# Opening of a two-block layer kernel on one core: x transposed before its norm, smaller first weight tiles, warm-up products

## The chip, the cores and the metric

The kernel runs on one core of a Trainium2 chip. The metric is the device time of one execution in microseconds (us). The core's engines are TensorE (PE, matrix products; its weight loads are listed as PEld), VectorE (DVE), ScalarE (ACT), GpSimd (POOL) and the queue of SyncE (SP), which here issues every transfer from memory. Each engine works through its own list of instructions in order and waits at an instruction until what it needs is there.

## The reference

A block of 256 tokens with 1024 features passes through two decoder layers and a second, different block. Only the start of the first layer bears on this change:

```python
def rmsnorm(x, g):
    y = xf * lax.rsqrt(jnp.mean(xf * xf, axis=-1, keepdims=True) + EPS)
    return (y * g).astype(x.dtype)
...
proj = rmsnorm(h, g_norm) @ w_in                # 1024 -> 6144
q, k, v, gate = jnp.split(proj, ...)            # 4 heads
q = rotary(heads(q, RET_QK_DIM), pos)
k = rotary(heads(k, RET_QK_DIM), pos) * (RET_QK_DIM ** -0.5)
o = retention_chunkwise(q, k, heads(v, RET_V_DIM))
...
y = (jax.nn.silu(gate) * o_normed) @ w_out
return h + y
...
gate = jax.nn.sigmoid(rmsnorm(h, g) @ w_gate)   # per layer embedding
return h + gate * (p_i @ w_emb)
```

The second block needs cosines and sines of the token positions (`positions_2`), which have nothing to do with the first layer.

## The kernel before, in words

All weights come from memory in tiles of up to 1 MB, in the order of a list (`make_plan`, L117). `Tile` (L161) issues a tile's load on the SP queue into one of three raw buffers; `split` (L173) cuts a half of it into two float32r parts, `hi` by ScalarE (L178) and `lo = raw - hi` by VectorE (L179), into one of four buffers each. A product of float32 accuracy is then three matmuls, hi*hi, hi*lo, lo*hi (`mm_A`, L250 to L255, 512 columns each). `gen_A` (L257) runs such products with tokens on the partitions and K outermost, two token halves to a weight tile; `ahead` (L197) splits the next tile's halves meanwhile. `gen_B` (L230) makes results with features on the partitions.

TensorE's order is the order of the program (`manual_schedule`, L278). The order of the other engines' lists is chosen when the program is built, by a scheduler, except inside blocks that name ScalarE and VectorE as manual too.

The opening goes so. `p`, two tiles of `ple_w_emb`, `x` in two halves of 128 tokens and the first tile of `ret_w_in` are asked for (L288 to L297, L171), then the tables `c_cos`, `c_sin`, `c_dec` (L617, L618). TensorE transposes `p` (`embed_T`, L413). `normed_all` (L388) takes the mean squares of `x`, one half on ScalarE (L392) and one on VectorE (L393); GpSimd turns each into 1/sqrt (`rstd`, L334: an add, L335, and a power, L336); VectorE multiplies `x` by it (L397). `embed` (L424) runs the 24 products p @ w_emb, and between its third and last quarter TensorE transposes the normed `x` (16 transposes, L362), which `split_psum` with the gain (L350, L351) brings into the operand `X`. Then come the gate and values of head 0 (L613: 96 matmuls, four 1 MB tiles), its queries and keys (`col_q`, `col_k`, L620), whose evacuation `ret_rope` (L476) multiplies by the tables `cs`, and the other heads.

`angles` (L556) is called after head 1's products. It loads the positions and the inverse frequencies (`posi`, L560; `inv`, L564) and reduces the angles on GpSimd: 45 small instructions, L562 to L591.

Of the kernel before, what the change touches and what calls it, by code (L numbers as in the profile page):

```python
# [17 lines left out]
P = 128  # L18
BIG = 1.0e30
T = 256  # L20
# [5 lines left out]
class Units:  # L26
    """4 KB per-partition slots; a freed slot is taken again in the order of release."""
# [31 lines left out]
class TPair:  # L59
    """A transposed operand [K = 4*128 per unit][tokens] as its two float32r parts."""  # L60
# [16 lines left out]
def build(nc, tc, A, out, stage=99):  # L77
# [27 lines left out]
    # ---------------------------------------------------------------- weights  # L105
    # The weights come in tiles of up to 1 MB, in the order of PLAN. A tile is loaded ahead of its
    # use and split into two float32r parts, hi + lo = the float32 value exactly.
# [9 lines left out]
    def make_plan():  # L117
        for n in range(2):
            plan_A("ple_w_emb", 0, [n * 512], 2, 2)
        plan_A("ret_w_in", 0, [4096, 2048])  # L120
# [40 lines left out]
    class Tile:  # L161
        """A tile of weights; h(k), l(k): the two parts of its K tile k"""

        def __init__(self, spec):
            key, lay, k0, nk, c0, ncol = self.spec = spec
            ap = A[key] if lay is None else A[key][lay]
            self.m, self.ncol, self.per = nk * ncol // 2, ncol, nk // 2
            self.hs, self.ls = [], []
            self.raw = wp.tile([P, 2048], F, tag="raw", bufs=3, name=nm("raw"))
            rv = self.raw[:, :nk * ncol].rearrange("p (k n) -> p k n", k=nk)  # L170
            nc.sync.dma_start(rv, ap[k0 * P:(k0 + nk) * P, c0:c0 + ncol].rearrange("(k p) n -> p k n", p=P))  # L171
# [25 lines left out]
    def ahead():  # L197
        """split one half more of the tile that comes next"""
# [21 lines left out]
    # Products come as generators that stop after every 6 matmuls of 512 columns (or 12 of 256),  # L220
    # so that other work of the tensor engine can be put in between.
# [8 lines left out]
    def gen_B(x, ap, c0, evac, ntiles=2, nk=8):  # L230
        """out[ntiles * 128 columns on partitions][256 tokens], two tiles to a bank; evac(i, bank)"""
# [25 lines left out]
    def gen_A(x, cols, evac, nk=8, kt=4):  # L257
        """out[tokens][512 columns of each (ap, c0)], K tiles outermost; evac(i, half, bank)"""
        ps = [[acc(), acc()] for _ in cols]
        for k0 in range(0, nk, kt):  # L260
            last = k0 + kt >= nk
            for i, (ap, c0) in enumerate(cols):
# [5 lines left out]
                for j, (k, h) in enumerate(order):  # L268
# [3 lines left out]
                    if j % 2 == 1:  # L272
                        if j // 2 in LOOK:
                            ahead()
# [5 lines left out]
    # ---------------------------------------------------------------- constants  # L280
# [10 lines left out]
    pn0 = embed_load(A["p"][0, 0])  # L291
    vret = cp.tile([8, P], F, name="vret")
    nc.sync.dma_start(vret, A["ret_norm"].rearrange("l (k p) -> (l k) p", p=P))
    loaded(2)
    nat = [U.get(), U.get()]
    for h in range(2):
        nc.sync.dma_start(nat[h].t, A["x"][0, h * P:(h + 1) * P, :])  # L297
# [35 lines left out]
    # ---------------------------------------------------------------- shared pieces  # L333
# [4 lines left out]
    def sumsq(src, dst, n):  # L338
        """dst[p] = mean over n of src^2, for the piece given"""
# [13 lines left out]
    def transpose_cols(src, kts, dsts):  # L353
        """src(h, k) -> [128 tokens, 128 columns]; dsts: list of (TPair, gcol or None)"""
# [21 lines left out]
    def normed(src, ss, eps):  # L376
        """src divided by its root mean square; ss: per half, the mean squares of its two pieces"""
# [10 lines left out]
    def normed_all(src, eps):  # L388
        """as normed, the sums of squares of the halves on two engines"""
        xn = [U.get(), U.get()]  # L390
        ss, rs = [small(1), small(1)], [small(1), small(1)]
        nc.scalar.activation(xn[0].t, src[0].t, AF.Square, scale=1.0 / 32.0, accum_out=ss[0])  # L392
        nc.vector.scalar_tensor_tensor(xn[1].t, src[1].t, 1.0 / 1024.0, src[1].t, OP.mult, OP.mult, accum_out=ss[1])  # L393
        for h in range(2):
            rstd(rs[h], ss[h], eps)
            for c in range(2):
                nc.vector.tensor_scalar(xn[h].t[:, c * 512:(c + 1) * 512], src[h].t[:, c * 512:(c + 1) * 512],  # L397
                                        rs[h], None, OP.mult)
        return xn

    class Flat:
        """An operand of up to two K tiles held in one unit, float32r parts side by side"""
# [21 lines left out]
    def embed(pu, w_ap, mid=None):  # L424
        """p @ w_emb, natural, two units; mid() goes before the last quarter of the products"""
# [22 lines left out]
    # ================================================================ retention  # L448
    with tc.manual_schedule(engines={mybir.EngineType.Activation, mybir.EngineType.DVE}):
        pu = embed_T(pn0)  # L450
        for i in range(4):
            queue[i // 2].split()
        vectors_T()
        xn = normed_all(nat, 1e-6)
    X = TPair(U, 8)
    emb = embed(pu, ("ple_w_emb", 0), lambda: transpose_cols(
        lambda h, k: xn[h].t[:, k * P:(k + 1) * P], list(range(8)), [(X, gcol("ret"))]))
    for u in xn:
        u.free()
# [4 lines left out]
    def ret_gv(hd):  # L464
        """evacuation of the gate (column group 0) and the values (1) of a head"""
# [3 lines left out]
        def gate(i, h, ps):  # L469
            nc.scalar.activation(sg.t[:, h * 512:(h + 1) * 512], ps, AF.Silu)  # L470

        def val(i, h, ps):
            split_psum(ps, vh.t[:, h * 512:(h + 1) * 512], vl.t[:, h * 512:(h + 1) * 512])
# [1009 lines left out]
```

## Time and profile before

| | |
|---|---|
| median of 3 runs | 891.42 us (891.24 to 891.92) |
| the profiled execution's own time | not listed with it; its span, first to last instruction, is 889.4 us |
| TensorE busy | 866.6 us, 97% of the span |
| VectorE, ScalarE, GpSimd busy | 620.4, 522.5, 68.4 us |
| mean rate of the transfers | 174 GB/s |

The span leaves out what lies before the first and after the last instruction; the median of the runs is 2.0 us above it. In the timeline each row is one instruction or a run of like ones: start, duration, engine, line, operation, result and inputs, count, and in brackets the idle time of its engine before it with what ended it. A matmul's duration includes its passage through the array, so the rate is read from the distance of two starts.

### The profile page before, as it was taken

How to read it: one execution, taken by the hardware profiler on the slowest of the kernel's cores; microseconds unless marked ns; L12 is line 12 of the kernel's file. 1: busy time of each engine (PE TensorE's matmuls, PEld its weight loads, DVE VectorE, ACT ScalarE, POOL GpSimd, SP SyncE). 2: the span in 40 equal slices, each digit the busy share in tenths (PEclk: the TensorE clock that was granted, in tenths of full speed). 3: DMA queues.
4: the chain of work that ended last, by engine and by line, in shares of the span. 5: the costliest groups of instructions: out<-in, count | busy, mean ns of one | idle time of the engine just before them, and what ended most of it. 6: DMA issues, size and time to landing. Idle time of an engine off the chain costs nothing.

```text
span 889.4 us, 14303 instructions
## 1 busy us (share of the span) xinstructions
PE 866.6 (97%) x5579; PEld 782.9 (88%) x5579; DVE 620.4 (70%) x1078; ACT 522.5 (59%) x948; POOL 68.4 (8%) x152
## 2 busy tenths in 40 slices
PE   6999999999999999999999999999999999999995
PEld 5889898888789999988988888787789999999994
DVE  5577677775687866887777656897857475446665
ACT  6554455454775767976968546647954545444441
POOL 2270000000100000000000000000023000000002
PEclk9999999999999999999999999999999999999998
DMA  8754545644466787425143553746455546655541
GB/s 284 239 190 150 182 148 171 220 143 166 156 212 190 231 298 238 118 78 180 55 143 114 176 187 128 236 150 218 154 160 173 190 142 191 202 184 190 182 142 48
DMA packets 115525, 154.69 MB, mean 174 GB/s; under 512 B 4737, under 2 KB 77826, under 8 KB 115458
## 3 DMA queue, kind: packets, MB, share of 16 engines
q1 hardware_dynamic: 115458, 153.78, 52.6%
q8 instruction: 44, 0.72, 0.3%
q14 instruction: 23, 0.19, 0.1%
HBM read 152.72 MB, written 1.05 MB: 173 GB/s over the span
## 4 chain that ended last, share of the span: by engine, by line
PE 62%; issue 3%; ACT 3%; DVE 2%; POOL 1%; POOLq 0%; ACTq 0%
PE acc L240 11%; PE acc L241 11%; PE acc L242 11%; PE acc L255 6%; PE acc L253 6%; PE acc L254 6%; ACT n L1159 1%; PE tps L1025 1%; ACT whi L178 1%; PE acc L796 1%; PE acc L795 1%; PE tps L362 1%; DVE wlo L179 1%; PE tps L1190 1%; PE acc L1012 1%
## 5 line engine op out<-in xcount | busy, mean ns | idle before, releaser
L179 DVE TENSOR_TENSOR wlo<-raw,whi 128x1024 fp32r<-128x1024 f32 (+1 forms) x284 | 339.0, 1201 | 169.2 <-ACT whi L178 168.4
L178 ACT ACTIVATE whi<-raw 128x1024 fp32r<-128x1024 f32 (+1 forms) x284 | 293.4, 1040 | 221.7 <-PE acc L241 99.8
L240 PE MATMUL acc<-n,whi 128*128 128x256 f32 x960 | 273.3, 285 | 0.0
L242 PE MATMUL acc<-n,wlo 128*128 128x256 f32 x960 | 271.7, 283 | 0.0
L241 PE MATMUL acc<-n,whi 128*128 128x256 f32 x960 | 271.5, 283 | 0.0
L253 PE MATMUL acc<-whi,n 128*128 128x512 f32 x568 | 225.6, 397 | 2.8 <-ACT whi L178 2.8
L254 PE MATMUL acc<-wlo,n 128*128 128x512 f32 x568 | 222.7, 392 | 0.3 <-DVE wlo L179 0.3
L255 PE MATMUL acc<-whi,n 128*128 128x512 f32 x568 | 222.4, 391 | 0.0
L241 PEld LDWEIGHTS acc<-n,whi 128*128 128x128 f32 x960 | 184.1, 192 | 0.6
L240 PEld LDWEIGHTS acc<-n,whi 128*128 128x128 f32 x960 | 183.9, 192 | 0.4
L242 PEld LDWEIGHTS acc<-n,wlo 128*128 128x128 f32 x960 | 184.0, 192 | 0.2 <-DVE wlo L179 0.2
L253 PEld LDWEIGHTS acc<-whi,n 128*128 128x128 f32 x568 | 107.4, 189 | 25.0 <-ACT whi L178 2.9
L255 PEld LDWEIGHTS acc<-whi,n 128*128 128x128 f32 x568 | 107.2, 189 | 23.1 <-DVE n L351 0.4
L254 PEld LDWEIGHTS acc<-wlo,n 128*128 128x128 f32 x568 | 107.4, 189 | 22.2 <-DVE wlo L179 1.2
L347 ACT ACTIVATE n<-tmp 128x512 fp32r<-128x512 f32 (+1 forms) x32 | 19.7, 615 | 40.5 <-DVE tmp L1017 11.9
L335 POOL TENSOR_SCALAR sm<-sm 128x1 f32<-128x1 f32 (+1 forms) x26 | 8.8, 337 | 421.9 <-DVE sm L1413 195.7
L980 ACT ACTIVATE n<-n,sm 128x16 f32<-128x16 f32 (+2 forms) x96 | 37.6, 393 | 0.8 <-DVE sm L978 0.4
L350 ACT ACTIVATE n<-tps,colv 128x256 fp32r<-128x256 f32 x64 | 27.1, 480 | 11.4 <-PE tps L362 6.3
L351 DVE SCALAR_TENSOR_TENSOR n<-tps,colv,n 128x256 fp32r<-128x256 f32 x64 | 28.0, 477 | 2.3 <-ACT n L350 1.8
L348 DVE TENSOR_TENSOR n<-tmp,n 128x512 fp32r<-128x512 f32 (+1 forms) x32 | 21.8, 681 | 10.0 <-ACT n L347 9.6
L348 DVE TENSOR_TENSOR n<-tps,n 128x512 fp32r<-128x512 f32 x31 | 20.6, 685 | 6.4 <-ACT n L347 6.2
L347 ACT ACTIVATE n<-tps 128x512 fp32r<-128x512 f32 x31 | 17.6, 591 | 10.5 <-PE tps L1025 6.1
(246 smaller groups left out, 845.9 us busy)
## 6 DMA issues: line engine op xcount, KB each, us to landing
raw<-in_w_in_dram SPq DMA_DIRECT2D x36, 1024.0 KB, 4.9
raw<-in_ret_w_in_dram SPq DMA_DIRECT2D x24, 1024.0 KB, 5.1
raw<-in_nsa_w_in_dram SPq DMA_DIRECT2D x16, 1024.0 KB, 5.2
raw<-in_kv_w_dram SPq DMA_DIRECT2D x12, 1024.0 KB, 5.0
raw<-in_ret_w_out_dram SPq DMA_DIRECT2D x8, 1024.0 KB, 4.9
raw<-in_ple_w_gate_dram SPq DMA_DIRECT2D x8, 1024.0 KB, 5.1
raw<-in_nsa_w_out_dram SPq DMA_DIRECT2D x8, 1024.0 KB, 5.1
raw<-in_cmp_w_k_dram SPq DMA_DIRECT2D x4, 1024.0 KB, 5.5
```

Source lines behind the costliest of these rows:

```text
L178: nc.scalar.activation(hi[:, :m], src, AF.Copy)
L179: nc.vector.tensor_tensor(lo[:, :m], src, hi[:, :m], OP.subtract)
L240: mm(o, wh, x.hi(k), start=(k == 0), stop=False)
L241: mm(o, wh, x.lo(k), start=False, stop=False)
L242: mm(o, wl, x.hi(k), start=False, stop=(k == nk - 1))
L253: mm(ps, xh, wh, start=start, stop=False)
L254: mm(ps, xh, wl, start=False, stop=False)
L255: mm(ps, xl, wh, start=False, stop=stop)
L347: nc.scalar.activation(hi, src, AF.Copy)
L348: nc.vector.tensor_tensor(lo, src, hi, OP.subtract)
L351: nc.vector.scalar_tensor_tensor(lo, src, scale, hi, OP.mult, OP.subtract)
L980: nc.scalar.activation(dst, dst, AF.Exp, bias=mx[:, i:i + 1], scale=-1.0, accum_out=sums[:, b * 3 + i:b * 3 + i + 1])
```

## The change

`normed_all` goes. `x` is transposed as it comes (`x_T`), its gain still applied when the transposes are brought out. The factor 1/rms of each token (`rsr`) is applied where it can be afterwards: as `scale` of the gate's Silu and of the values' evacuation, for all four heads, and for queries and keys by multiplying it into the tables `cs`. For that `rsr` is spread over 128 columns by VectorE (L665), transposed by TensorE (L666), and multiplied into `cs` (L668). The two mean squares are taken later, in the midst of head 0's products (L647, L648). The embedding's weights come as two tiles of one K tile each; head 0's gate and value weights as eight tiles of 0.5 MB (`kt=2`) in place of four of 1 MB. Five products of the identity with itself stand ahead of `embed_T` and three behind it (`warm`). The tables and small vectors are asked for behind the fifth 0.5 MB tile. Core of the diff:

```diff
-        for n in range(2):
-            plan_A("ple_w_emb", 0, [n * 512], 2, 2)
-        plan_A("ret_w_in", 0, [4096, 2048])
+        PLAN.extend(("ple_w_emb", 0, k, 1, 0, 1024) for k in range(2))
+        plan_A("ret_w_in", 0, [4096, 2048], kt=2)
...
-                        if j // 2 in LOOK:
+                        if kt == 2 or j // 2 in LOOK:
                             ahead()
...
+    with tc.manual_schedule(engines={mybir.EngineType.SP}):
+        pn0 = embed_load(A["p"][0, 0])
+        loaded(1)
+        nc.sync.dma_start(vret, A["ret_norm"].rearrange("l (k p) -> (l k) p", p=P))
+        for h in range(2):
+            nc.sync.dma_start(nat[h].t, A["x"][0, h * P:(h + 1) * P, :])
+        loaded(3)
+    def warm(n):
+        t = tps()
+        for i in range(n):
+            mm(t[:, i % 4 * P:(i % 4 + 1) * P], ident, ident, start=True, stop=True)
...
+    def x_T():
+        banks = [tps() for _ in range(4)]
+        for h in range(2):
+            for k in range(8):
+                c = k % 2 * 256 + h * P
+                nc.tensor.transpose(banks[k // 2][:, c:c + P], nat[h].t[:, k * P:(k + 1) * P], ident)
+        def evac(i):
+            for j in range(2):
+                k = 2 * i + j
+                split_psum(banks[i][:, j * 256:(j + 1) * 256], X.hi(k), X.lo(k), gcol("ret")(k))
+        return evac
...
-            nc.scalar.activation(sg.t[:, h * 512:(h + 1) * 512], ps, AF.Silu)
+            nc.scalar.activation(sg.t[:, h * 512:(h + 1) * 512], ps, AF.Silu, scale=rsr[:, h:h + 1])
-            split_psum(ps, vh.t[:, h * 512:(h + 1) * 512], vl.t[:, h * 512:(h + 1) * 512])
+            split_psum(ps, vh.t[:, h * 512:(h + 1) * 512], vl.t[:, h * 512:(h + 1) * 512], rsr[:, h:h + 1])
...
+    t = gen_A(X, [(wi, 4096), (wi, 2048)], lambda i, h, ps: (g, v)[i](i, h, ps), kt=2)
+    with tc.manual_schedule(engines={mybir.EngineType.Activation, mybir.EngineType.DVE}):
+        warm(5)
+        pu = embed_T(pn0)
+        warm(3)
+        ps = [[acc(), acc()], [acc(), acc()]]
+        def emb_out(n):
+            for h in range(2):
+                nc.scalar.activation(emb[h].t[:, n * 512:(n + 1) * 512], ps[n][h], AF.Copy)
+        for k in range(2):
+            if k:
+                vectors_T()
+                evac = x_T()
+                evac(0)
+                evac(1)
+                queue[0].split()
+                evac(2)
+                queue[0].split()
+                evac(3)
+            w = load_w("ple_w_emb", 0, k, 1, 0, 1024)
+            for n in range(2):
+                for h in range(2):
+                    mm_A(ps[n][h], Flat(pu), k, h, w.h(n), w.l(n), k == 0, k == 1)
+        ahead()
+        emb_out(0)
+        ahead()
+        emb_out(1)
+        adv(t, 5)
+        ss = [small(1), small(1)]
+        j = [U.get(), U.get()]
+        nc.scalar.activation(j[0].t, nat[0].t, AF.Square, scale=1.0 / 32.0, accum_out=ss[0])
+        nc.vector.scalar_tensor_tensor(j[1].t, nat[1].t, 1.0 / 1024.0, nat[1].t, OP.mult, OP.mult, accum_out=ss[1])
+        for h in range(2):
+            j[h].free()
+            rstd(rsr[:, h:h + 1], ss[h], 1e-6)
+    pu.free()
+    adv(t, 2)
...
+    with tc.issue_after(queue[-1].dma.ins):
...
+    run(t)
+
+    rb, rp = tmp(), tps()
+    for h in range(2):
+        nc.vector.tensor_copy(rb[:, h * P:(h + 1) * P], rsr[:, h:h + 1].to_broadcast([P, P]))
+        nc.tensor.transpose(rp[:, h * P:(h + 1) * P], rb[:, h * P:(h + 1) * P], ident)
+    for i in range(2):
+        nc.vector.tensor_tensor(cs[:, i, :], cs[:, i, :], rp[:, :256], OP.mult)
```

Three lists show where the scheduler puts things now. First the SP queue, from its first transfer; `n_..` are the 4 KB units (`p`, `x`, tables), `raw_..` the weight tiles. Before:

```order
L288 DMA n_1_82<-in_p_dram 128x2x256
L293 DMA vret<-in_ret_norm_dram 8x128
L171 DMA raw_86<-in_ple_w_emb_dram 128x2x512
L171 DMA raw_88<-in_ple_w_emb_dram 128x2x512
L297 DMA n_2_90<-in_x_dram 128x1024
L297 DMA n_3_91<-in_x_dram 128x1024
L171 DMA raw_218<-in_ret_w_in_dram 128x4x512
L617 DMA n_16_380<-in_c_cos_dram 128x256
```

and in the change:

```order
L288 DMA n_3_87<-in_p_dram 128x2x256
L171 DMA raw_89<-in_ple_w_emb_dram 128x1024
L296 DMA vret<-in_ret_norm_dram 8x128
L298 DMA n_1_82<-in_x_dram 128x1024
L298 DMA n_2_83<-in_x_dram 128x1024
L171 DMA raw_94<-in_ple_w_emb_dram 128x1024
L171 DMA raw_96<-in_ret_w_in_dram 128x2x512
L563 DMA posi<-in_positions_dram 128x2x1
L567 DMA inv<-in_c_inv_dram 128x32
L171 DMA raw_241<-in_ret_w_in_dram 128x2x512
```

The positions and inverse frequencies moved up from the 25th and 26th place of the queue to the 8th and 9th, straight behind the first 0.5 MB tile.

GpSimd, behind the constants that it sets up at the start: `sm_..` are the two mean squares and their 1/sqrt, L562 on is `angles`. Before:

```order
L335 TENSOR_SCALAR sm_131<-sm_129 128x1
L336 TENSOR_TENSOR sm_131<-sm_131,mhalf 128x1
L335 TENSOR_SCALAR sm_132<-sm_130 128x1
L336 TENSOR_TENSOR sm_132<-sm_132,mhalf 128x1
L562 CAST posf<-posi 128x2
L568 TENSOR_SCALAR n_28_900<-inv,posf 128x32 x2
```

In the change `CAST posf<-posi` (L565) follows the constants directly, the 45 instructions of `angles` run in one piece, and their last two rows stand ahead of the 1/sqrt:

```order
L590 TENSOR_TENSOR trig<-trig,n_28_956 128x64
L594 TENSOR_SCALAR trig<-trig 128x64
L343 TENSOR_SCALAR rsr<-sm_291 128x1
L344 TENSOR_TENSOR rsr<-rsr,mhalf 128x1
L343 TENSOR_SCALAR rsr<-sm_292 128x1
L344 TENSOR_TENSOR rsr<-rsr,mhalf 128x1
```

The two pieces changed places: the 1/sqrt of `x` came before `angles` and now comes after all of it.

VectorE in the change, in head 0's gate and value products; `raw_96`, `raw_241`, `raw_263`, `raw_285`, `raw_318`, `raw_354` are the first to sixth of the eight 0.5 MB tiles, two splits each:

```order
L179 TENSOR_TENSOR wlo_266<-raw_263,whi_265 128x512
L179 TENSOR_TENSOR wlo_276<-raw_263,whi_275 128x512
L179 TENSOR_TENSOR wlo_288<-raw_285,whi_287 128x512
L648 SCALAR_TENSOR_TENSOR n_15_294,sm_292<-n_2_83 128x1024
L179 TENSOR_TENSOR wlo_309<-raw_285,whi_308 128x512
L179 TENSOR_TENSOR wlo_321<-raw_318,whi_320 128x512
L665 COPY tmp_442<-rsr 128x128 x2
L179 TENSOR_TENSOR wlo_345<-raw_318,whi_344 128x512
L179 TENSOR_TENSOR wlo_357<-raw_354,whi_356 128x512
```

The two copies that spread `rsr`, which the program writes behind head 0, stand between the two splits of the fifth tile. From the end of head 0 on, the lists of all engines are those of before, but for the scaled evacuations of the four heads, the two transposes (L666) and the two products into `cs` (L668).

## Rows read from the trace of the kernel before

**Rows 1.** The page's head and part 1: busy us (share of span), instructions of each engine.

```profile
span 889.4 us, 14303 instructions
...
PE 866.6 (97%) x5579; PEld 782.9 (88%) x5579; DVE 620.4 (70%) x1078; ACT 522.5 (59%) x948; POOL 68.4 (8%) x152
```

**Rows 2.** TensorE's waits in 0 to 80 us: line, releaser, us in total, times, longest.

```profile
PE tps L419 <- DMA n<-in_p_dram: 3.7, 1, 3.7
...
PE acc L253 <- ACT whi L178: 2.8, 1, 2.8
```

**Rows 3.** TensorE's timeline: start us, us, engine, line, operation, out<-in, count.

```profile
7.85 0.80 PE L253 MATMUL acc<-whi,n 128*128 128x512 f32 x1 [2.83 <-ACT whi L178]
...
8.57 0.80 PE L254 MATMUL acc<-wlo,n 128*128 128x512 f32 x1
...
13.01 0.63 PE L255 MATMUL acc<-whi,n 128*128 128x512 f32 x1
...
13.44 0.49 PE L253 MATMUL acc<-whi,n 128*128 128x512 f32 x1
...
14.93 1.91 PE L362 MATMUL tps<-ident,n 128*128 128x128 f32 x16
...
18.05 0.39 PE L253 MATMUL acc<-whi,n 128*128 128x512 f32 x1
...
18.73 0.39 PE L253 MATMUL acc<-whi,n 128*128 128x512 f32 x1
...
40.49 0.28 PE L240 MATMUL acc<-n,whi 128*128 128x256 f32 x1
```

**Rows 4.** The SP queue's issues in the timeline.

```profile
5.79 0.58 SPq L617 DMA_DIRECT2D n<-in_c_sin_dram  x1
...
32.59 0.50 SPq L560 DMA_DIRECT2D posi<-in_positions_dram  x1
```

**Rows 5.** Transfers issued in 0 to 60 us: size, us from issue to landing.

```profile
n<-in_c_sin_dram SPq DMA_DIRECT2D x1, 128.0 KB, 8.5
...
posi<-in_positions_dram SPq DMA_DIRECT2D x1, 1.0 KB, 4.7
```

**Rows 6.** GpSimd's timeline: the piece `angles` and a later 1/sqrt.

```profile
37.39 0.71 POOL L562 CAST posf<-posi 128x2 f32<-128x2 int32 x1 [23.30 <-DMA posi<-in_positions_dram]
...
39.64 0.24 POOL L576 CAST n<-ni 128x64 f32<-128x64 int32 x1
...
40.70 1.11 POOL L579 CAST n<-ni 128x64 f32<-128x64 int32 x1
...
52.20 1.27 POOL L576 CAST n<-ni 128x64 f32<-128x64 int32 x1
...
59.37 1.36 POOL L586 TENSOR_SCALAR n<-n 128x64 f32<-128x64 f32 x1
...
63.81 0.43 POOL L591 TENSOR_SCALAR trig<-trig 128x64 f32<-128x64 f32 x1
...
71.02 0.22 POOL L335 TENSOR_SCALAR sm<-sm 128x1 f32<-128x1 f32 x1 [6.78 <-DVE sm L526]
...
71.33 0.57 POOL L336 TENSOR_TENSOR sm<-sm,mhalf 128x1 f32<-128x1 f32 x1
```

**Rows 7.** VectorE's timeline: splits, a sum of squares, a copy.

```profile
7.83 2.65 DVE L179 TENSOR_TENSOR wlo<-raw,whi 128x512 fp32r<-128x512 f32 x4 [1.66 <-ACT whi L178]
...
11.07 1.25 DVE L393 SCALAR_TENSOR_TENSOR n<-n 128x1024 f32<-128x1024 f32 x1 [0.52 <-DMA n<-in_x_dram]
...
52.15 1.23 DVE L179 TENSOR_TENSOR wlo<-raw,whi 128x1024 fp32r<-128x1024 f32 x1 [0.20 <-ACT whi L178]
...
54.49 0.21 DVE L327 COPY colv<-tps 128x57 f32<-128x57 f32 x1
```

**Rows 8.** Stretches: length, busy PE, PEld, DVE, ACT, POOL (instructions), clock granted, DMA share, GB/s.

```profile
880.00:881.00 1.00, 0.35 (x2) 0.00 (x0) 0.67 (x2) 0.00 (x0) 0.34 (x1) 1.00 0.00 0
...
885.00:886.00 1.00, 0.00 (x0) 0.00 (x0) 0.00 (x0) 0.00 (x0) 0.70 (x1) 0.50 0.00 0
```

More of the change, by code (lines that the diff above doesn't have):

```diff
@@ L166, in __init__ @@
             ap = A[key] if lay is None else A[key][lay]
-            self.m, self.ncol, self.per = nk * ncol // 2, ncol, nk // 2
+            self.m, self.ncol, self.per = nk * ncol // 2, min(ncol, 512), max(nk // 2, 1)
             self.hs, self.ls = [], []
@@ L170, in __init__ @@
             rv = self.raw[:, :nk * ncol].rearrange("p (k n) -> p k n", k=nk)
-            nc.sync.dma_start(rv, ap[k0 * P:(k0 + nk) * P, c0:c0 + ncol].rearrange("(k p) n -> p k n", p=P))
+            self.dma = nc.sync.dma_start(rv, ap[k0 * P:(k0 + nk) * P, c0:c0 + ncol].rearrange("(k p) n -> p k n", p=P))
         def split(self):
@@ L289, in embed_load @@
         return pn
-    pn0 = embed_load(A["p"][0, 0])
+    nat = [U.get(), U.get()]
     vret = cp.tile([8, P], F, name="vret")
[L293 to L297, printed above, removed]
+    with tc.manual_schedule(engines={mybir.EngineType.SP}):
[9 more added lines that the diff above has]
+            mm(t[:, i % 4 * P:(i % 4 + 1) * P], ident, ident, start=True, stop=True)
     vecs = cp.tile([P, P], F, name="vecs")
@@ L386, in normed @@
         return xn
[L388 to L399, printed above, removed]
     class Flat:
@@ L446, in dump @@
         es.close()
[L449 to L454, printed above, removed]
-    X = TPair(U, 8)
[L456 to L459, printed above, removed]
+    X = TPair(U, 8)
+    emb = [U.get(), U.get()]
+    rsr = cp.tile([P, 2], F, name="rsr")
+    def x_T():
[9 more added lines that the diff above has]
+        return evac
     wi = ("ret_w_in", 0)
@@ L612, in build @@
     g, v = ret_gv(0)
-    run(gen_A(X, [(wi, 4096), (wi, 2048)], lambda i, h, ps: (g, v)[i](i, h, ps)))
+    t = gen_A(X, [(wi, 4096), (wi, 2048)], lambda i, h, ps: (g, v)[i](i, h, ps), kt=2)
[33 more added lines that the diff above has]
+            rstd(rsr[:, h:h + 1], ss[h], 1e-6)
@@ L614, in build @@
+    pu.free()
+    adv(t, 2)
     cs_u, dec_u = U.get(), U.get()
     cs, dec = cs_u.v(2, 256), dec_u.v(4, 256)
-    for i, c in enumerate(("c_cos", "c_sin")):
-        nc.sync.dma_start(cs[:, i, :], A[c])
-    nc.sync.dma_start(dec, A["c_dec"].rearrange("h p n -> p h n"))
-    vectors2_load()
+    with tc.issue_after(queue[-1].dma.ins):
+        for i, c in enumerate(("c_cos", "c_sin")):
+            nc.sync.dma_start(cs[:, i, :], A[c])
+        nc.sync.dma_start(dec, A["c_dec"].rearrange("h p n -> p h n"))
+        vectors2_load()
```

## The prediction, made before any run of the change

> **What bounds the kernel now.** The page first: TensorE is busy 866.6 of 889.4 us [rows 1], so a change pays only where it moves TensorE. The waits of TensorE come next: in the first 80 us it waits 3.7 us for `p` and 2.8 us for the first split weights [rows 2], and hardly at all for anything else. In its timeline [rows 3] the reader is to see three points. The embedding starts at 7.85 us and runs from 8.57 us on. From 8.57 to 13.44 us eleven matmuls of 512 columns take 4.87 us, a start every 0.43 us, which is 1.2 GHz; later three starts take 0.68 us (18.05 to 18.73), 0.227 us each, the level of 2.4 GHz. Eleven at that pace take 2.5 us, so the low clock costs 2.4 us. Head 0's gate and value products (96 matmuls) start at 18.05 us, and its queries at 40.49 us. That second point is my yardstick, because from there on TensorE's list is the same in both kernels, apart from two transposes.
>
> **What the change sets out to do** is to fill the idle time before 7.85 us, and to take the sums of squares, the 1/sqrt and the multiplication out of the way of X. None of those held TensorE up for long: it has work from 8.57 to 18.05 us. At the very most the change gains the 2.4 us of low clock and the 0.6 us that head 0 now takes beyond 96 x 0.227 = 21.8 us.
>
> **What it adds.** The lists above decide. GpSimd now runs all of `angles` before the 1/sqrt of `x`, and VectorE has the two copies of `rsr` between the two splits of the fifth 0.5 MB tile of head 0. VectorE works in order: at the first copy it stands until GpSimd has done `angles` and the 1/sqrt, and behind it stands the second `lo` part of the fifth tile, which TensorE needs. So I add up when that part is ready.
>
> 1. *The positions arrive.* On the one queue transfers land in the order of their issue. Before, 2308 KB (p, the norm gain, two embedding tiles, x) are through when VectorE takes the second half of x at 11.07 us [rows 7]. The sines, 1280 KB later in the queue, are issued at 5.79 us and land 8.5 us later, at 14.3 us [rows 4, 5]: 512 KB take 1.3 us. The change puts 2820 KB ahead of the positions, so these come at about 11.07 + 1.3 = 12.4 us, and the first instruction of `angles` starts at 12.5 us. The positions' own transfer is small (4.7 us from issue to landing before, behind a tile).
>
> 2. *`angles` itself.* Before, it runs from 37.39 to 64.24 us, 26.85 us for 45 instructions [rows 6]. Eight of them take 1.05 to 1.36 us, 9.9 us in all, where the same operations take 0.24 to 0.37 us elsewhere (L576: 1.27 us at 52.20, 0.24 us at 39.64). The one at 52.20 us lies beside VectorE's split of 52.15 to 53.38 us and ends just behind it [rows 7]; the other seven lie so too. Each costs 0.93 us, so a split of 1.23 us costs GpSimd its length less 0.3 us. Without these 7.4 us, 19.4 us are left. In the change VectorE has eleven half splits of 0.66 us (2.65 us for four [rows 7]) and one sum of squares of 1.25 us between 12.5 us and the copy: 11 x 0.36 + 0.95 = 4.9 us. Bounds: 0, if the short splits fall between GpSimd's instructions; 8.5 us, if each costs its full length. I take 4.9 us, nearest to the rows. `angles` then ends at 12.5 + 19.4 + 4.9 = 36.8 us.
>
> 3. *The 1/sqrt and the copies.* An add and a power take 0.88 us from start to end (71.02 to 71.90 us [rows 6]); two such pairs, 1.8 us. The second copy takes about 0.2 us (a copy of 128x57 takes 0.21 us [rows 7]), the split 0.7 us. Ready: 39.5 us.
>
> 4. *TensorE's way from there.* Left are 41 of the 96 matmuls: five of the fifth tile's second half, and 36. At 0.227 us that is 9.3 us. It has idled before: it comes to this place 54 matmuls, 12.2 us, after head 0 begins. That beginning lies between 18 us (embedding at the high clock) and 20.5 us (at the low one, with a wait of about 2 us for the evacuated X and the second tile, which ScalarE now splits behind four evacuations), so it stands from 30 to 33 us until 39.5 us. At the end of the kernel TensorE has its last matmul before 881 us, and in the stretch from 885 us the granted clock is 0.50, the level of 1.2 GHz [rows 8]; in the opening, after an idle time of under 3 us, the matmuls ran at that level too. So it starts low again. Bounds: 0 if the clock holds, and 2.4 us as in the opening; I take 2.4 us, since the idle time is the longer of the two. The two transposes of L666 cost 0.2 us (sixteen take 1.91 us [rows 3]). The queries begin at 39.5 + 9.3 + 2.4 + 0.2 = 51.4 us.
>
> The sum: 51.4 - 40.5 = 10.9 us later. The profiled execution has a span of 889.4 us, the median of the runs is 2.0 us above it, and nothing around the span changes: 891.4 + 10.9 = **902.3 us**.
>
> **What costs nothing.** The eight warm-up products lie before 7.85 us, where TensorE waits in any case; whatever they do to the clock, the time won is spent in the wait for the fifth tile. The same hides the waits for X, the later sums of squares, and the eleven transfers of tables and vectors that now stand between the fifth and the sixth tile on the queue; without that wait the sixth tile would be the next thing late. The seventh tile's load is not touched, but the eighth's waits for the late split; it has 29 matmuls' time, over 6 us, more than the 4.7 us that the positions took behind a 1 MB tile [rows 5]. The scaled evacuations and the two products into `cs` run beside TensorE's queries and keys. The dropped multiplications gave VectorE time that it had.
>
> **A rule against the trace.** The rows say that a split holds GpSimd up for its length less 0.3 us. The Trainium skill (SBUF — State Buffer, section Who interferes with whom) says that a VectorE instruction with two inputs in SBUF and a GpSimd instruction that reads SBUF exclude each other, whichever starts first holding the port for its whole instruction. If GpSimd were always the second and lost the full length each time, the hold-up would be 8.5 us in place of 4.9 us, and the sum 905.9 us. That is the third rival below.
>
> **The rivals.**
> - *Faster: TensorE never stands at the fifth tile, and the warm-up works.* Then head 0 could begin 2.4 us sooner, at 15.65 us, and the queries 21.8 + 0.2 us later, at 37.7 us: 2.8 us gained, 888.6 us. For it: the idle time is there and the low clock is real. Against it: VectorE would need `rsr` by 15.65 + 12.2 - 0.9 = 27 us, 12 us sooner than the sum has it; even with no hold-up at all it is there at 34 us. Chance 0.04.
> - *The wait is met, but short: GpSimd is not held up by the half splits and the clock stays high.* 10.9 - 4.9 - 2.4 = 3.6 us, 895.0 us. For it: the half splits are short; against it: all eight rows of the same meeting. Chance 0.12, with the cases between.
> - *Every split costs its full length:* 905.9 us. Eight of eight rows show 0.3 us less. Chance 0.12.
> - *The opening loses a little and no more* (X waits for its evacuation, head 0 begins at 20.5 us, no stand at the copy): the queries at 40.0 to 42.5 us, 0.5 us faster to 2.0 us slower, which counts as no change. It needs the same early `rsr` as the first. Chance 0.04.
> - That the warm-up leaves the clock low is likely enough, but has no price here: the end of the wait is GpSimd's.
>
> **How the numbers follow.** The sum has 0.68. The range reaches from the short wait, with the positions up to 1 us sooner, 894.0 us, to the full hold-up with half a us more, 906.5 us. A measurement of this kernel tells about 0.2% (1.8 us) from no change. All cases but the first and the fourth are slower by more: slower 0.92, within 0.2% 0.04, faster 0.04.
>
> **What would show it.** In the profile of the changed kernel: GpSimd's first cast near 12.5 us, the last instruction of `angles` near 37 us, VectorE idle from about 27 us to 38.6 us and then the copies; TensorE's longest wait, 7 to 9 us, at L254 for `wlo`, with starts 0.43 us apart behind it, and the queries from about 51 us. I am wrong if the positions land much later or earlier, if TensorE goes through the fifth tile without standing, or if the stretch behind 51 us differs in length from that behind 40.5 us before.

## The result and the profile after

| | before | with the change |
|---|---|---|
| median | 891.33 us (890.97 to 891.92, 4 runs) | 902.34 us (901.87 to 902.55, 4 runs) |
| ratio, 95% interval | | 1.0123 [1.0109, 1.0136] |
| the profiled execution: own time, span | span 889.4 us | 902.22 us, 900.1 us |
| queries begin (TensorE) | 40.49 us [rows 3] | 49.67 us |

The change costs 11.0 us, where 10.9 us were forecast (902.3 us). Part of that agreement is luck: the mechanism is the one forecast, but several of its terms were off, and their errors cancel.

The waits of TensorE in the first 80 us of the changed kernel, the view of [rows 2] (line, releaser, us in total, times, longest):

```profile
PE acc L254 <- DVE wlo L179: 4.7, 4, 3.8
PE acc L253 <- ACT whi L178: 3.4, 3, 2.9
PE tps L305 <- POOL ident masks.py:199: 1.5, 1, 1.5
PE acc L242 <- DVE wlo L179: 0.4, 1, 0.4
```

The wait for `p` (3.7 us in [rows 2]) is filled but for 1.5 us, in which TensorE waits for the identity matrix `ident` that the warm-up multiplies. New are 3.8 us for one `lo` part, the forecast place, and 2.9 us for one `hi` part. TensorE's timeline (start us, us, engine, line, operation, count, idle time before with its releaser), to be laid beside [rows 3]:

```profile
6.11 0.50 PE L253 MATMUL acc<-whi,n 128*128 128x512 f32 x1 [0.21 <-ACT whi L178]
...
7.25 0.39 PE L255 MATMUL acc<-whi,n 128*128 128x512 f32 x1
7.48 0.40 PE L253 MATMUL acc<-whi,n 128*128 128x512 f32 x1
...
14.63 0.50 PE L253 MATMUL acc<-whi,n 128*128 128x512 f32 x1 [2.87 <-ACT whi L178]
...
15.73 0.63 PE L255 MATMUL acc<-whi,n 128*128 128x512 f32 x1
16.16 0.63 PE L253 MATMUL acc<-whi,n 128*128 128x512 f32 x1
...
19.61 0.40 PE L253 MATMUL acc<-whi,n 128*128 128x512 f32 x1
...
33.31 0.39 PE L253 MATMUL acc<-whi,n 128*128 128x512 f32 x1
37.52 0.79 PE L254 MATMUL acc<-wlo,n 128*128 128x512 f32 x1 [3.82 <-DVE wlo L179]
38.12 0.63 PE L255 MATMUL acc<-whi,n 128*128 128x512 f32 x1
38.54 0.63 PE L253 MATMUL acc<-whi,n 128*128 128x512 f32 x1
...
43.14 0.40 PE L255 MATMUL acc<-whi,n 128*128 128x512 f32 x1
43.37 0.40 PE L253 MATMUL acc<-whi,n 128*128 128x512 f32 x1
...
49.67 0.36 PE L240 MATMUL acc<-n,whi 128*128 128x256 f32 x1
```

Read the distance of the starts. The warm-up works in this execution: from 7.25 us on, the products start 0.23 us apart, the level of 2.4 GHz, where before they ran 0.43 us apart [rows 3]. The gain is lost at once: TensorE stands 2.87 us before the second embedding tile, and the next products run at 1.2 GHz again. Head 0 begins at about 19.6 us (18.05 before). Then comes the stand at the second split of head 0's fifth tile, until 37.52 us, and thirteen starts at or near the low level behind it.

What this split waits for: GpSimd's timeline (first row of `angles`, two of its others, its last, then the first and last of the two 1/sqrt pairs; rows of before: [rows 6]) and VectorE's ([rows 7]).

```profile
12.43 0.19 POOL L565 CAST posf<-posi 128x2 f32<-128x2 int32 x1 [9.39 <-DMA posi<-in_positions_dram]
...
26.56 1.11 POOL L582 CAST n<-ni 128x64 f32<-128x64 int32 x1
...
31.52 0.69 POOL L589 TENSOR_SCALAR n<-n 128x64 f32<-128x64 f32 x1
...
34.42 0.24 POOL L594 TENSOR_SCALAR trig<-trig 128x64 f32<-128x64 f32 x1
34.74 0.23 POOL L343 TENSOR_SCALAR rsr<-sm 128x1 f32<-128x1 f32 x1
...
36.05 0.56 POOL L344 TENSOR_TENSOR rsr<-rsr,mhalf 128x1 f32<-128x1 f32 x1
```

```profile
31.23 0.74 DVE L179 TENSOR_TENSOR wlo<-raw,whi 128x512 fp32r<-128x512 f32 x1 [3.02 <-ACT whi L178]
35.66 0.23 DVE L665 COPY tmp<-rsr 128x128 f32<-128x128 f32 x1 [3.69 <-POOL rsr L344]
36.64 0.23 DVE L665 COPY tmp<-rsr 128x128 f32<-128x128 f32 x1 [0.75 <-POOL rsr L344]
36.78 0.68 DVE L179 TENSOR_TENSOR wlo<-raw,whi 128x512 fp32r<-128x512 f32 x1
```

This is the forecast chain link by link: positions, 45 instructions, two pairs, two copies, one split. It ends at 37.46 us instead of 39.5. The SP queue holds a second thing that is late: the sixth tile is issued behind the tables, and ScalarE's split of it begins only at 37.13 us.

```profile
24.69 0.43 SPq L659 DMA_DIRECT2D n<-in_c_dec_dram  x1
...
33.01 0.90 SPq L171 DMA_DIRECT2D raw<-in_ret_w_in_dram  x2
```

### The profile page after: what moved, and what is told of

Same layout as the page of the kernel before. It is cut to its first block, busy times and chain, and to the rows that moved or that the text cites. A ratio compares the mean times of both kernels' runs of the same rounds, so it can differ in the third digit from the quotient of the medians.

```text
span 900.1 us, 14376 instructions
## 1 busy us (share of the span) xinstructions
PE 873.6 (97%) x5597; PEld 787.4 (87%) x5597; DVE 621.1 (69%) x1086; ACT 524.9 (58%) x956; POOL 62.6 (7%) x152
## 4 chain that ended last, share of the span: by engine, by line
PE 83%; ACT 5%; DVE 4%; issue 4%; DMA 2%; POOL 1%; SPq 0%; POOLq 0%; ACTq 0%; DVEq 0%
PE acc L242 13%; PE acc L240 13%; PE acc L241 13%; PE acc L254 11%; PE acc L255 11%; PE acc L253 11%; DVE wlo L179 2%; ACT whi L178 2%; ACT n L1208 1%; DMA raw<-in_ret_w_in_dram 1%; PE tps L370 1%; PE tps L1074 1%; DMA n<-in_c_dec_dram 1%; PE acc L845 1%; PE acc L844 1%
## 5 line engine op out<-in xcount | busy, mean ns | idle before, releaser
L240 PE MATMUL acc<-n,whi 128*128 128x256 f32 x960 | 273.4, 285 | 0.0
L242 PE MATMUL acc<-n,wlo 128*128 128x256 f32 x960 | 271.9, 283 | 0.5 <-DVE wlo L179 0.4
L253 PE MATMUL acc<-whi,n 128*128 128x512 f32 x568 | 226.4, 399 | 3.4 <-ACT whi L178 3.4
L255 PE MATMUL acc<-whi,n 128*128 128x512 f32 x568 | 223.2, 393 | 0.0
L242 PEld LDWEIGHTS acc<-n,wlo 128*128 128x128 f32 x960 | 184.0, 192 | 1.1 <-DVE wlo L179 1.1
L240 PEld LDWEIGHTS acc<-n,whi 128*128 128x128 f32 x960 | 183.9, 192 | 0.4
L253 PEld LDWEIGHTS acc<-whi,n 128*128 128x128 f32 x568 | 107.7, 190 | 26.6 <-ACT whi L178 4.3
L255 PEld LDWEIGHTS acc<-whi,n 128*128 128x128 f32 x568 | 107.6, 189 | 23.2 <-DVE n L359 0.5
L355 ACT ACTIVATE n<-tps 128x512 fp32r<-128x512 f32 x31 | 17.7, 592 | 10.3 <-PE tps L1074 6.1
```

Of the source, the lines that this page charges most:

```text
L240: mm(o, wh, x.hi(k), start=(k == 0), stop=False)
L242: mm(o, wl, x.hi(k), start=False, stop=(k == nk - 1))
L253: mm(ps, xh, wh, start=start, stop=False)
L255: mm(ps, xl, wh, start=False, stop=stop)
L355: nc.scalar.activation(hi, src, AF.Copy)
```

## The experiments

Theory: GpSimd's order (all of `angles` ahead of the 1/sqrt), carried to TensorE by VectorE's copies, sets the end of the opening; whatever makes TensorE arrive there sooner or later, as long as it comes before about 37.5 us, has no price. The rivals: the place of the tables on the queue, the later opening, the warm-up. In the expectations "the eighth split" means this same stand, which is at the second split of the *fifth* tile (the tenth of head 0's splits), and "the sixth experiment" means all three edits with the warm-up, which is part of 7 below. Line numbers differ by a few between the kernels: L255 to L257 of some are L253 to L255 of the change, and L242 to L244 are its L240 to L242.

| run | edit to the change | median us | against the change |
|---|---|---|---|
| change | | 902.34 | |
| order | 1/sqrt before `angles` | 900.35 | -2.0 |
| copies | copies of `rsr` later on VectorE | 899.98 | -2.4 |
| tables | tables earlier on the queue | 901.99 | -0.4 |
| order + tables | both | 894.91 | -7.4 |
| no warm-up | eight products out | 902.30 | 0.0 |
| early splits only | order of splits and evacuations | 900.98 | -1.4 |
| order + tables + early splits | | 890.30 | -12.0 |
| the same without warm-up | | 891.63 | -10.7 |
| the same with warm-up, tiles ahead | | 888.92 | -13.4 |

The kernel before was 891.58 to 891.73 us beside these. All kernels but order + tables and the last three ran four times, with a spread of up to 4.4 us (order, 899.36 to 903.77 us): the 0.4 us of the tables is not clear of that spread, nor by the times alone is the 2.0 us of the order or the 1.4 us of the early splits. There the argument rests on the traces.

**1. The order on GpSimd.**

```diff
-            rstd(rsr[:, h:h + 1], ss[h], 1e-6)
+            last_rstd = rstd(rsr[:, h:h + 1], ss[h], 1e-6)
...
-            angles()
+            with tc.issue_after(last_rstd.ins):
+                angles()
```

> Edit: on GpSimd the program of `angles` is issued behind the two 1/sqrt pairs, so the norm factor no longer waits for it; all else as in the change. Theory A (the order on GpSimd is the whole wait): the factor is ready soon after the sums of squares, near 29 to 32 us, the 3.8 us wait of TensorE on the eighth split goes, and with it the low clock behind it (2.4 us): some 6 us less, about 896 us. Theory B (a second thing is late at almost the same time: the sixth tile of head 0 was only issued at 33.0 us, behind the tables' transfers, and landed at 37.0): TensorE stops at the next tile instead, resumes at about 38, the low clock stays, and 0.3 to 1.5 us are won, 901 to 902 us.

Measured: 900.35 us (899.36 to 903.77), ratio to before 1.0105 [1.0084, 1.0125]. Theory B, with 0.5 us more than it allowed. The profiled execution is the slowest of the four (903.77 us), so its rows show the place and not the usual size. TensorE's timeline at the stand, and the SP queue's:

```profile
39.39 0.79 PE L253 MATMUL acc<-whi,n 128*128 128x512 f32 x1 [3.50 <-ACT whi L178]
```

```profile
34.59 0.39 SPq L171 DMA_DIRECT2D raw<-in_ret_w_in_dram  x1
```

The factor is ready at 31.7 us here, TensorE goes through the fifth tile, and stands one tile later, where the sixth tile's transfer waits behind the tables. The stand has changed its releaser from `wlo` to `whi`, and the time has hardly moved.

**2. The copies on VectorE.** GpSimd's order stays; the copies are put behind the last split of the eighth tile.

```diff
-        nc.vector.tensor_copy(rb[:, h * P:(h + 1) * P], rsr[:, h:h + 1].to_broadcast([P, P]))
+        with tc.issue_after(TILES["ret_w_in", 0, 6, 2, 2048, 512].lo_ins.ins):
+            nc.vector.tensor_copy(rb[:, h * P:(h + 1) * P], rsr[:, h:h + 1].to_broadcast([P, P]))
```

> Edit: GpSimd's order stays as in the change, but VectorE's two copies of the norm factor are issued behind the second split of the eighth tile, so nothing on VectorE that TensorE needs stands behind the factor. Theory A (the copies in VectorE's queue are what passes GpSimd's lateness on to TensorE): the 3.8 us wait on that split goes, though the factor is still ready only near 36 us; if nothing else is late then, some 6 us less, 896 us. Theory B (the sixth tile, issued behind the tables, is late next): 901 to 902 us, as for the order on GpSimd. Rival to both: the gate's and values' evacuations need the factor too and stop TensorE at the same place; then 902 us with the wait on a bank.

Measured: 899.98 us (899.22 to 900.79), ratio 1.0096 [1.0079, 1.0113]. That is 1 us less than theory B allowed. The factor is later than in the change (the last power ends at 37.9 us, 36.6 there), and the 3.8 us wait for `wlo` is gone all the same. So it is the copies' place in VectorE's list that hands GpSimd's lateness to TensorE. What comes next is again the sixth tile: a wait of 2.6 us until 36.20 us, for ScalarE's split. No wait for a bank shows, so the evacuations do not stop TensorE.

**3. The place of the tables, and 4. both together.**

```diff
-    with tc.issue_after(queue[-1].dma.ins):
+    with tc.issue_after(TILES["ret_w_in", 0, 0, 2, 2048, 512].dma.ins):
```

> Edit: the transfers of the rotary and decay tables and of the norm vectors are issued behind the second tile of head 0, not behind its fifth; GpSimd and VectorE as in the change. Theory A and B agree that GpSimd still sets the end of the wait: the eighth split stands behind the copies until about 37.5, so 902 us within 0.6. If instead the tables' place alone was the cost, the sixth tile would land before 34 us and the time would fall to about 896 us. If the earlier tables take bandwidth from the first tiles of head 0, the start is later by up to 2 us.

> Edit: both the order on GpSimd and the place of the tables (the first and the third experiment together). Theory B: only both together free TensorE; the 3.8 us wait and the low clock behind it go, queries begin at 43 to 44 us, and the time is 895 to 897 us; the rest to the kernel before (about 4 to 5 us) is the later opening. Theory A: no better than the order alone. A third view, that TensorE's lost time is made up later by waits in the queries, gives 899 us or more.

Measured: the tables alone 901.99 us (901.73 to 903.19), ratio 1.0119 [1.0104, 1.0134]; both 894.91 us (893.99 to 895.32), ratio 1.0035 [1.0022, 1.0048]. TensorE's waits from 12 to 60 us, first the longest of the tables alone, then the longest of both:

```profile
PE acc L256 <- DVE wlo L179: 5.4, 2, 5.2
```

```profile
PE acc L255 <- ACT whi L178: 2.9, 1, 2.9
```

Apart, the two edits win 2.0 and 0.4 us; together 7.4 us, which is theory B (895 to 897 us), if a little more. That is the mark of two waits that end at about the same time: taking one away uncovers the other. With both gone, TensorE is busy for all of 30 to 40 us at full clock (second row; the first is the change):

```profile
30.00:40.00 10.00, 5.55 (x17) 3.63 (x17) 3.78 (x7) 2.93 (x5) 5.42 (x15) 0.81 0.47 144
```

```profile
30.00:40.00 10.00, 10.00 (x45) 8.26 (x45) 4.95 (x8) 5.67 (x8) 8.63 (x19) 1.00 0.85 262
```

(length; busy PE, PEld, DVE, ACT, POOL with their instructions; granted clock; DMA share; GB/s). The queries begin at 41.74 us, 7.9 us earlier than in the change and 1.3 us later than before. Of the 3.2 us that are left to the kernel before, 1.3 us lie ahead of the queries, where the 2.9 us before the second embedding tile remain; the rest lies behind their beginning.

**5. Without the warm-up.**

```diff
-        warm(5)
...
-        warm(3)
```

> Edit: the change without its eight warm-up products. Theory (in the change, TensorE's opening is no bound: it stops before the eighth split until about 37.5 us whenever it arrives before that): the first products run at the low clock again, TensorE reaches the eighth split 0.5 to 2.4 us later and waits that much less there; 902 us within 0.7, as the change. Rival (the wait is counted from where TensorE arrives, so that a later opening is paid in full): 903 to 904.7 us.

Measured: 902.30 us (901.89 to 902.97), ratio 1.0119 [1.0105, 1.0133], the change's own time. TensorE's timeline:

```profile
16.41 0.49 PE L253 MATMUL acc<-whi,n 128*128 128x512 f32 x1 [2.87 <-ACT whi L178]
...
38.15 0.79 PE L254 MATMUL acc<-wlo,n 128*128 128x512 f32 x1 [3.91 <-DVE wlo L179]
```

The second embedding tile starts 1.8 us later than in the change, and nothing of it is left at the end. It is not made good as the theory had it, by a shorter wait: TensorE reaches the stand 0.5 us later, and the stand ends 0.6 us later too, since GpSimd's chain does (why was not tried). Fewer products at the low level behind it make up for that (see the last section), so the 0.0 us is partly luck.

**6. Early splits, alone.** ScalarE and VectorE take the second embedding tile and head 0's first two tiles ahead of most evacuations of x.

```diff
+                loaded(3)
+                queue[0].split()
+                queue[0].split()
                 evac(0)
+                queue[1].split()
                 evac(1)
-                queue[0].split()
-                evac(2)
-                queue[0].split()
-                evac(3)
+                queue[1].split()
...
+        evac(2)
+        evac(3)
+        adv(t, 3)
+        evac(4)
+        evac(5)
+        adv(t, 2)
+        evac(6)
+        evac(7)
```

(`evac` takes one K tile here, not two; each `emb_out` is followed by a split of head 0's second tile. `loaded(3)` asks for one more tile at this point. In the change ScalarE waits four times, 0.55 to 0.82 us each, for VectorE's part of one K tile before it takes the next; here a split of weights fills such a gap.)

> Edit: the change with the early splits of the sixth experiment alone; GpSimd's order and the tables' place as in the change. Theory (GpSimd sets the end of the wait, whenever TensorE arrives): TensorE arrives some 5 us earlier and stands some 5 us longer, 902 us within 1. Rival (the slow opening is what the change lost): 897 us. Should the two tables of transfers follow the fifth tile earlier, GpSimd's chain still ends at 36 to 37 us.

Measured: 900.98 us (900.37 to 902.55), ratio 1.0106 [1.0092, 1.012].

```profile
27.16 0.39 PE L253 MATMUL acc<-whi,n 128*128 128x512 f32 x1
...
29.09 0.50 PE L253 MATMUL acc<-whi,n 128*128 128x512 f32 x1 [0.40 <-ACT whi L178]
37.88 0.80 PE L254 MATMUL acc<-wlo,n 128*128 128x512 f32 x1 [8.29 <-DVE wlo L179]
```

The stand is not at the same split as in the change. The fifth tile's second split needs no wait here; the copies come behind it in VectorE's list, and TensorE stands six products later, at the `lo` part of the sixth tile's first split. The product that stands last before the wait in the change (33.31 us there) starts at 27.16 us, 6.2 us sooner. TensorE then does six products more, stands 8.3 us in place of 3.8, and goes on at the same time within 0.4 us: the earlier opening brings no earlier end of the stand. The queries begin at 47.45 us, 2.2 us sooner than in the change, and this is the sum of three things: six products (1.4 us) are already done, 1.2 us less are lost to the low clock (last section), and the stand ends 0.4 us later. So the median, 900.98 us, just below the 901 us that the theory allowed, does not show a price of the later opening at the same wait: the wait moved. At the very stand of the change, the tables alone give the same test, smaller: TensorE comes 1.2 us sooner (last product ahead of it at 32.13 us), stands 5.2 us, and goes on 0.2 us later.

In the four kernels that stand at the copies, TensorE's start follows the end of GpSimd's last power by the same 0.91 us, however long it stood. That power in the early splits alone, and TensorE's starts around the stand in the tables alone (the other starts and the change's power stand above, the rest in the table):

```profile
36.41 0.56 POOL L344 TENSOR_TENSOR rsr<-rsr,mhalf 128x1 f32<-128x1 f32 x1
```

```profile
32.13 0.39 PE L255 MATMUL acc<-whi,n 128*128 128x512 f32 x1
37.69 0.79 PE L256 MATMUL acc<-wlo,n 128*128 128x512 f32 x1 [5.17 <-DVE wlo L179]
```

| kernel | power ends | TensorE goes on | idle before |
|---|---|---|---|
| the change | 36.61 | 37.52 | 3.8 |
| tables | 36.78 | 37.69 | 5.2 |
| early splits alone | 36.97 | 37.88 | 8.3 |
| no warm-up | 37.24 | 38.15 | 3.9 |

**7. All three, with and without warm-up.** Early splits on top of order and tables.

> Edit: the fourth experiment (order on GpSimd, place of the tables), and on ScalarE and VectorE the splits of the second embedding tile and of head 0's first two tiles ahead of most of the evacuations of the transposed x, which lie between the later splits. Theory: the 2.9 us in which TensorE stood before the second embedding tile and the low clock behind it go, head 0 begins near 15 us rather than 20, queries begin near 38.5, and the time is 889.5 to 891.5 us, at or below the kernel before (891.7). Rival 1 (another thing holds the opening at 20 us: the weights' landing, with three raw buffers): 893.5 to 895 us. Rival 2 (an earlier head 0 meets the norm factor or the sixth tile late again): 891.5 to 894 us with a new wait between 28 and 36 us.

> Edit: the sixth experiment without the eight warm-up products. Theory: here the opening is on the path, so the warm-up shows its price: the first twelve products run 0.43 apart instead of 0.23, x's transposes begin up to 2.4 us later, and the time is 1 to 2.4 us above the sixth experiment. Rival (the low level before x lands costs nothing, because x's landing at 9.7 us is the next bound): within 0.5 us of the sixth experiment.

Measured: 890.30 us (889.38 to 891.37, 11 runs), ratio 0.9985 [0.9976, 0.9994]; without the eight products 891.63 us (890.84 to 893.68, 11 runs), ratio 1.0000 [0.9991, 1.0008]. Both times are as expected. With the stand gone the opening is on the path: the early splits, worth 1.4 us in the change, are worth 4.6 us here, and the warm-up, worth nothing there, is worth 1.3 us by the medians. TensorE's waits from 12 to 60 us of the kernel with the warm-up are only these:

```profile
PE acc L242 <- ACT whi L178: 0.9, 1, 0.9
PE acc L244 <- DVE wlo L179: 0.8, 1, 0.8
```

They stand at the first query tile, which is issued at 27.82 us, lands 9.1 us later, and is split by ScalarE from 37.02 us on. Where the warm-up's 1.3 us lie, no profile shows. Without the eight products the transposes of x start at 11.42 us instead of 10.10, but the two profiled executions (890.90 us with them, 890.98 without) meet this same tile: its split begins at 37.02 us in both, and the first product with a `lo` part of it starts at 39.38 and 39.40 us. In these two the query tile hides the gain.

**8. The tiles of head 0 ahead.** Its eight 0.5 MB tiles go into free 4 KB units, not into the three raw buffers.

```diff
-            self.raw = wp.tile([P, 2048], F, tag="raw", bufs=3, name=nm("raw"))
+            self.unit = U.get() if nk * ncol == 1024 and key == "ret_w_in" else None
+            self.raw = self.unit.t if self.unit else wp.tile([P, 2048], F, tag="raw", bufs=3, name=nm("raw"))
...
-        loaded(3)
+        loaded(10)
```

> Edit: the sixth experiment, and head 0's eight half-size tiles are loaded into eight free units of the data buffers, so that all are issued at the start and the three raw buffers hold the query tiles sooner. In the sixth experiment the first query tile was issued at 27.8 us and its split began at 37.0, with TensorE standing 0.9 and 0.8 us before the queries. Theory: the transfers, which moved 186 GB/s between 20 and 30 us there, run on without gaps, the query tile lands before 30 us, both waits go, and 1.2 to 1.8 us are won: 888.5 to 889.1 us. Rival 1: TensorE meets the next buffers (the four split buffers) instead: within 0.5 us of the sixth experiment, 890.3. Rival 2: eight transfers at once slow the second embedding tile and x, and the opening loses 0.5 to 2 us: 890.8 to 892 us.

Measured: 888.92 us (888.59 to 890.36, 9 runs), ratio 0.9972 [0.9962, 0.9982]: 0.3% faster than the kernel before. In the stretch from 20 to 30 us the transfers move 251 GB/s instead of 186 (first the kernel of 7 with warm-up, then this one):

```profile
20.00:30.00 10.00, 9.93 (x44) 7.87 (x43) 8.21 (x17) 7.15 (x14) 4.94 (x9) 1.00 0.60 186
```

```profile
20.00:30.00 10.00, 9.84 (x44) 7.83 (x43) 8.32 (x17) 7.25 (x14) 3.16 (x4) 1.00 0.81 251
```

```profile
36.88 0.38 PE L676 MATMUL tps<-ident,tmp 128*128 128x128 f32 x2
37.01 0.36 PE L245 MATMUL acc<-n,whi 128*128 128x256 f32 x1
```

The last two rows are TensorE's: the queries follow the two transposes without a wait, 3.5 us before those of the kernel before [rows 3]; 2.7 us of that are left at the end. ScalarE splits the first query tile at 34.91 us instead of 37.02. The scheduler moved the positions back with this edit (issued at 26.56 us, first cast of `angles` at 35.27 us, 28.17 us without it), so more than the place of the tiles differs.

## Why the prediction was right, point by point

- **The cause.** The wait at VectorE's copies of `rsr`, behind GpSimd's `angles`, was forecast with its place and its line. Run 2 (copies) shows it, which removes the wait with GpSimd as late as ever, and so do the four kernels of the table, in which TensorE goes on 0.91 us behind GpSimd's last power, though it stands 3.8 to 8.3 us. Undoing the order alone won only 2.0 us, since the sixth tile, which the prediction named as the next thing late, was late at nearly the same time.
- **Step 1** (positions at 12.4 us, first cast at 12.5): 12.43 us. The first tile of head 0, issued at 3.54 us, landed after 8.6 us and the positions, issued at 4.10 us, after 8.3 us, in the order of their issue, as the step takes it.
- **Step 2** was mis-sized: `angles` took 22.2 us, not 24.3, and ended at 34.66 us, not 36.8. The hold-up was nearly right. L589 at 31.52 us takes 0.69 us beside the split of 31.23 to 31.97 us, and 0.37 us elsewhere, 0.32 us more (0.36 forecast). Beside the longer sum of squares L582 takes 1.11 us, beginning at 26.56 us, 0.25 us after it, 0.87 us more than elsewhere (0.95 forecast). Counted so, against the shortest time of the same instruction in the traces, twelve of the 45 are longer, by 4.3 us together (4.9 forecast), and each lies beside one of the eleven half splits or the sum of squares. The wrong term is the 19.4 us that were left from before. The same count gives 9.1 us of hold-up in the kernel before, 7.4 of them in the eight rows that the forecast took out. The other 1.7 us it left in, for instance in the first cast (0.71 us in [rows 6], 0.19 us here). The third rival, that every split costs its whole length, fell: 4.3 us, not 8.5. The Trainium skill (SBUF — State Buffer, section Who interferes with whom) states that a VectorE instruction with two inputs in SBUF contends with a GpSimd instruction that reads SBUF; the trace agrees, as these rows show.
- **Step 3** (1.8 us for the pairs, 0.9 for copy and split): 1.9 us and 0.8 us. The split was ready at 37.46 us.
- **Step 4**: the 41 products took from 37.52 to 49.53 us, 12.0 us, so the low clock cost 2.7 us where 2.4 were taken. The place where it was most wrong is TensorE's arrival, 33.5 us instead of 30 to 33: head 0 began at 19.6 us as allowed, but the fifth tile then came late (ScalarE waited for its transfer until 30.57 us). So the stand was 3.8 us, not the 7 to 9 named as its mark. It doesn't enter the sum, which counts from the end of the wait; that is why it did no harm.
- **Not in the sum**: the queries begin 9.2 us later than before (10.9 forecast), but the first score products are 10.3 us later, as the next two rows show, before and after (the 16 products of L500, which is L503 now; first and last start):

```profile
L500 PE MATMUL tps<-n,n x16: 277/283/283, 60.6 to 172.4; 128*128 128x256 f32 x16
```

```profile
L503 PE MATMUL tps<-n,n x16: 277/283/283, 70.9 to 182.7; 128*128 128x256 f32 x16
```

  The yardstick was wrong by 1.1 us. The first query tile is late as well: TensorE takes its two `lo` parts at 50.52 us, after a wait of 0.36 us, and at 52.31 us, each when VectorE's split of it ends (50.47 and 52.26 us), and behind that the distance to the kernel before no longer grows:

```profile
50.52 0.39 PE L242 MATMUL acc<-n,wlo 128*128 128x256 f32 x1 [0.36 <-DVE wlo L179]
...
52.31 0.39 PE L242 MATMUL acc<-n,wlo 128*128 128x256 f32 x1
```

```profile
49.24 1.23 DVE L179 TENSOR_TENSOR wlo<-raw,whi 128x1024 fp32r<-128x1024 f32 x1 [3.62 <-ACT whi L178]
...
51.04 1.22 DVE L179 TENSOR_TENSOR wlo<-raw,whi 128x1024 fp32r<-128x1024 f32 x1
```

  ScalarE begins this tile at 48.15 us, right behind the gate's evacuations (46.99 us). Whether its own list or the tile's transfer, issued only at 39.11 us, held it is not shown. From the first scores to the last nothing changes (111.8 us in both). A further 0.4 us lie behind the last product. In sum 9.2 + 1.1 + 0.4 = 10.7 us of span: the too long step 2 (-2.1) and the waits left out (+1.5) and the clock (+0.3) cancel. The 0.3 us from there to the 11.0 us of the medians are not explained.
- **What costs nothing**: the warm-up (0.0 us, fifth run) and the tables' transfers, with the warning that the sixth tile would be the next thing late; the first run shows exactly that.
- **The rivals**: the first named 27 us as the time by which VectorE would need the factor, and 888.6 us as the reward. The last run comes out there, 888.92 us, with the second power done at 28.1 us, and it took four edits more to get there. Its way there is another than this rival's: the queries begin at 37.01 us (37.7 in the rival), and 0.8 us of that lead are lost again. The short wait (895.0 us) did not come, since hold-ups (4.3 us) and low clock (2.7 us) were both real.

## What to carry to other kernels

When a change lets a scheduler place an independent piece of slow work, look in each engine's list at what now stands behind it: here 22 us of small GpSimd instructions for a later block went ahead of a factor that VectorE wants in the midst of the opening, and, with a late transfer that ended at the same time, cost 7.4 us, more than the whole change could gain. Before undoing the one wait that the profile shows, look for the next thing that is late at the same time; edits worth 2.0 and 0.4 us alone were worth 7.4 us together. And judge a warm-up only where its stretch is on the path: the same eight products were worth 0.0 us in one kernel and 1.3 us, by the medians, in another. When an edit moves a wait, count the products up to it before calling it the same wait.

## What was not expected of the hardware

The price of a stand in clock is not one number. Counted from the first product behind the stand to the first start back at 0.23 us, less 0.227 us for each, six stands cost 1.5 to 3.0 us:

| kernel | idle before, us | products start low, us | us lost |
|---|---|---|---|
| early splits alone | 8.3 | 37.88 to 40.92, 7 intervals | 1.5 |
| no warm-up | 3.9 | 38.15 to 41.63, 8 intervals | 1.7 |
| copies | 2.6 | 36.20 to 40.07, 8 intervals | 2.1 |
| tables | 5.2 | 37.69 to 42.96, 12 intervals | 2.5 |
| the change | 3.8 | 37.52 to 43.14, 13 intervals | 2.7 |
| order | 3.5 | 39.39 to 45.37, 13 intervals | 3.0 |

(The 2.1 us of the copies hold a further wait of 0.2 us for a `lo` part.) The longest stand cost least, so the idle time alone doesn't tell the price. What sets it was not tried.

Nor does the warm-up bring the high level every time. Eight profiles here have the same eight products. In six the products start 0.23 us apart from about 7.25 us on, in one (all three edits) from 7.80 us, and in that of the order the first products start 0.43 us apart:

```profile
6.73 0.79 PE L253 MATMUL acc<-whi,n 128*128 128x512 f32 x1 [0.55 <-ACT whi L178]
...
8.05 0.63 PE L255 MATMUL acc<-whi,n 128*128 128x512 f32 x1
8.47 0.63 PE L253 MATMUL acc<-whi,n 128*128 128x512 f32 x1
```

Why was not tried. What a warm-up is worth is therefore read from several executions, not from one profile.
